# One transfer brings a row block and all 1024 columns of an adaLN vector, whose four column quarters are summed over eight row blocks in one PSUM bank

## The chip, the cores and the metric

One core of a Trainium2 chip runs the whole program. The metric is the device time of one execution in microseconds. TensorE (PE) multiplies, VectorE (DVE) and ScalarE (ACT) work on elements, GpSimd (POOL) does some of the rest, and the queue of SyncE (SP) issues nearly all transfers. Each engine works through its own row of instructions in the order in which they were put there.

## The reference, cut to what matters

A backbone of two layers over 512 latent tokens and 256 context tokens, 1024 wide, all in float32. Each layer has nine modulation vectors for the latents (from `c`) and nine for the context (from `c_ctx`):

```
ml = jnp.split(jax.nn.silu(c) @ mod_w[l] + mod_b[l], 9, axis=-1)       # mod_w[l]: 1024 x 9216
mc = jnp.split(jax.nn.silu(c_ctx) @ mod_w[l] + mod_b[l], 9, axis=-1)
x = x + 0.5 * ml[2] * _swiglu(_modnorm(x, norm_g[l, 0], ml[0], ml[1]), ffn_w1[l, 0], ffn_w2[l, 0])
...
def _modnorm(h, g, shift, scale): return _rmsnorm(h, g) * (1.0 + scale) + shift
```

Vectors 0, 3 and 6 of a layer shift, 1, 4 and 7 scale, and 2, 5 and 8 are gates, for the first FFN, the mixer and the second FFN. Layer 0 mixes with RWKV-7 and S5 scans, layer 1 with windowed attention. The context stream ends with its keys and values in layer 1.

## The kernel before, in words

Activations stand feature-major, as [128, 8, tokens]. A dense product holds a 128x128 block of weights and moves 256 or 512 tokens over it; `weight` (L349) brings the weights by SP, ScalarE rounds them to a high part (L328) and VectorE makes the low part (L329), and `mm3` (L365) multiplies three times for each block, on lines 370, 371 and 372. Weight transfers are named `wraw`.

The modulation vectors are made by `mod` (L208). The two conditioning vectors, context and latent, stand after silu in `sc` (L180), 32 columns wide with zeros beside them, so that one product serves both. `mod_w` is 75.5 MB in all, 18 vectors of 1024x1024. The kernel before goes by quarters of a vector's columns (`ch`, 256 columns each). For a quarter it brings four transfers `wt` (L222) of two row blocks and 256 columns each, 256 KB in rows of 1 KB:

```
for q in range(4):
    wt = self.mw.tile([128, 2, 256], F32, tag="mw", name="wt")
    nc.sync.dma_start(out=wt, in_=w[:, 2 * q:2 * q + 2, c0:c0 + 256])
    for r in range(2):
        nc.tensor.matmul(ps[32 * q:32 * q + 32, :256], self.sc[:, 2 * q + r, 2 - i:34 - i], wt[:, r, :], ...
```

The stationary side is 32 columns of `sc`, so a matmul takes one of four quarters of the array's columns and writes 32 partitions of PSUM. Transfer q's two matmuls (L224) go to the same partitions 32q to 32q+31; the four partial sums of a column block then stand on four partition groups. ScalarE copies them out (L228), two products with a selection matrix `sel` (L230) add the four and turn them into columns, and VectorE adds the bias (L234) and, for scales and gates, one step more (L237, L239). Up to three vectors share one bank (`i`, for calls with a tuple of vectors).

Vectors 0 and 1 of layer 0 come first, alone (`M_0` = 20 buffers); vectors 2, 3 and 4 are woven into the context's first FFN (`M_A` = 6 buffers), the next ten of both layers into the stage in which the context and the latents run as two streams (`M_B` = 2 buffers), and the last three into the two FFNs between the layers (4 buffers). `weave` (L1505) takes steps from several generators in turn, by the cost that each step yields. The program is built by a planner (`TCOPT`) that then orders each engine's instructions by its own costs, so that a line's place in the code doesn't fix its place in an engine's row.

Of the kernel before, what the change touches and what calls it, by code (L numbers as in the profile page):

```python
# [8 lines left out]
F32 = mybir.dt.float32  # L9
# [29 lines left out]
AHEAD = 3000  # L39
W_B = (2, 4)  # L40
M_B = 2
M_A = 6
LATE = (3, 20)
M_0 = 20
F_MOD = 1.8
F_LAT = 1.4
F_CTX = (2.4, 2.2)
# [13 lines left out]
class Net:  # L61
# [107 lines left out]
    def mod_vectors(self, pool):  # L169

        nc, a = self.nc, self.a
        self.vec, self.modv = {}, {}
        self.rows("vec0", [
            ("cc", a["c_ctx"].rearrange("(r p) -> r p", p=128)),
            ("c", a["c"].rearrange("b (r p) -> (b r) p", p=128)),
            ("mod_b0", a["mod_b"][0].rearrange("(r p) -> r p", p=128)),
            ("norm_g0", a["norm_g"][0].rearrange("s (r p) -> (s r) p", p=128)),
        ], pool)

        sc = self.const.tile([128, KB, 34], F32, name="sc")  # L180
# [3 lines left out]
        self.sc = sc  # L184

        self.sel = self.const.tile([128, 6], F32, name="sel")
        nc.vector.tensor_reduce(out=self.sel, in_=self.ident.rearrange("p (q i) -> p i q", q=4)[:, 0:6, :],
                                axis=mybir.AxisListType.X, op=ALU.add)

    def vectors(self, pool):  # L190
        a = self.a
# [13 lines left out]
        self.rows("vec2", [("mod_b1", a["mod_b"][1].rearrange("(r p) -> r p", p=128))], pool)  # L205


    def mod(self, l, *vs):  # L208

        nc = self.nc  # L210
        w = self.a["mod_w"][l].rearrange("(k p) n -> p k n", p=128)
        nv = len(vs)
        dst = self.const.tile([128, KB, nv, 2], F32, name=f"mod{l}_{vs[0]}")
        col = lambda nm, v, ks: self.vec[f"{nm}{l}"][:, v * KB + ks.start:v * KB + ks.stop].rearrange(
            "p (k i) -> p k i", i=1).to_broadcast([128, 2, 2])
        for ch in range(4):
            ps = self.bank("psmod") if self.start else self.norm_psum()
            for i, v in enumerate(vs):
                c0 = v * D + ch * 256
                for q in range(4):  # L220
                    wt = self.mw.tile([128, 2, 256], F32, tag="mw", name="wt")
                    nc.sync.dma_start(out=wt, in_=w[:, 2 * q:2 * q + 2, c0:c0 + 256])  # L222
                    for r in range(2):
                        nc.tensor.matmul(ps[32 * q:32 * q + 32, :256], self.sc[:, 2 * q + r, 2 - i:34 - i], wt[:, r, :],  # L224
                                         start=(i == 0 and r == 0), stop=(i == nv - 1 and r == 1))
                yield 3
            m = self.mw.tile([128, 256], F32, tag="modp", bufs=self.mp_bufs, name="modp")
# [3 lines left out]
            ks = slice(2 * ch, 2 * ch + 2)  # L231
            for i, v in enumerate(vs):
                o = dst[:, ks, i, :]
                nc.vector.tensor_tensor(out=o, in0=ps[:, 256:268].rearrange("p (k i v) -> p v k i", k=2, v=3)[:, i],  # L234
                                        in1=col("mod_b", v, ks), op=ALU.add)
                if v % 3 == 1:
                    nc.vector.scalar_tensor_tensor(out=o, in0=o, scalar=1.0, in1=col("norm_g", v // 3, ks), op0=ALU.add, op1=ALU.mult)  # L237
                elif v in (2, 8):
                    nc.vector.tensor_scalar(out=o, in0=o, scalar1=0.5, scalar2=None, op0=ALU.mult)  # L239
        for i, v in enumerate(vs):  # L240
            self.modv[l, v] = dst[:, :, i, :]


    def load_x(self, src, dst, pool):
# [14 lines left out]
    def sq_add(self, k, grp):  # L259

        nc = self.nc
        c0, n = grp
        if k == 0:
            self.ssum = getattr(self, "ssum", {})
            self.ssum[grp] = self.tp.tile([128, n], F32, tag=f"ss{c0}", bufs=1, name="ss")
            nc.scalar.activation(out=self.ssum[grp][:, :n], in_=self.xs(k, grp), func=ACTF.Square)
        else:
            sq = self.tp.tile([128, 256], F32, tag=f"sq{int(c0 >= CTX)}", bufs=1, name="sq")
            nc.scalar.activation(out=sq[:, :n], in_=self.xs(k, grp), func=ACTF.Square)
            nc.vector.tensor_tensor(out=self.ssum[grp][:, :n], in0=self.ssum[grp][:, :n], in1=sq[:, :n], op=ALU.add)  # L270

# [74 lines left out]
                                           in1=h[0][:, k, :].bitcast(F32), op0=ALU.add, op1=ALU.subtract)  # L346


    def weight(self, ap, pool=None, bufs=None):  # L349

        nc = self.nc
        _, kk, n = ap.shape
# [165 lines left out]
    def ab_tile(self, j, hs, consume, pool):  # L518

        c = slice(128 * j, 128 * j + 128)  # L520
        w, = self.weight(self.a["ab_in_w"][0].rearrange("(k p) n -> p k n", p=128)[:, :, c], pool, (1, self.ibufs[3]))
        for i, h in enumerate(hs):
            n = h[0].shape[2]
            ps = self.bank("pab")
# [969 lines left out]
def late(t, gen):  # L1494
    yield t
    yield from gen
# [8 lines left out]
def weave(*gens):  # L1505
    run(weave_gen(*gens))
# [16 lines left out]
def dit_kernel(ctx: ExitStack, tc: tile.TileContext, args, out):  # L1523
# [17 lines left out]

    def mods(l, *vs):
        for v in vs:
            yield from net.mod(l, *(v if isinstance(v, tuple) else (v,)))

    def scaled(gen, f):
        for t in gen:
# [95 lines left out]
    with net.psum(*PS), left("mix") as mp:  # L1643
        with net.mod_weights(M_A), net.weights(5, 5), right("r1") as rp:
# [10 lines left out]
            def more():  # L1655
# [10 lines left out]
            weave(ffn(0, 0, C, rp, FF_A), (late(LATE[0], mods(0, 2, (3, 4))), F_MOD), more())  # L1666
        with net.mod_weights(M_B), net.weights(*W_B):
            weave(ctx_stream(), lat_stream(), (chain(mods(0, (5, 6, 7), 8), mods(1, (0, 1, 2), (3, 4, 5))), 8.5))
    kp = ctx.enter_context(left("kv"))
    with net.psum(0, 2, m=4):  # L1670
        net.attn_setup()
        net.attn_tiles(kp)
        hc = tuple(xs.enter_context(right("hc" + p)).tile([128, KB, CTX], F32R, name=f"hc{p}") for p in "hl")
        with net.weights(*W_E, "left"), net.mod_weights(4), left("l12") as lp:
            def both():

                nh = []
# [16 lines left out]
            weave(both(), late(345, chain(mods(1, (6, 7, 8)), ctx_kv())))  # L1694
        xs.close()
    with net.psum(0, 2, 0, 2):
        late_w = ctx.enter_context(ExitStack())
# [61 lines left out]
```

## Time and profile before

| | |
|---|---|
| median of 3 runs | 3461.26 us (3457.91 to 3472.96) |
| the profiled execution | 3468.21 us, span 3466.4 us, mean granted clock 0.981 |
| PE busy, weight loads | 3362.3 us (97%), 2842.8 us (82%) |
| DVE, ACT, POOL busy | 1930.0 (56%), 1343.6 (39%), 331.8 us (10%) |
| moved | 463 MB, 134 GB/s over the span |
| transfers of `mod_w` | 288 of 256 KB |

A row of the timeline or of a group names line, engine, operation and tiles as out<-in. A float32 matmul that isn't rounded, as on line 224, leaves two records, its two passes. A matmul's duration includes its way through the array, so that records overlap; how fast PE works is read from start to start. All times are microseconds from the span's start.

### The profile page before, as it was taken

The page shows a single profiled execution, that of the slowest core. Times are in us where ns is not written, and L with a number is a line of the kernel's source. Part 1 is how long each engine was busy: PE and PEld are TensorE (multiplying, and loading weights), DVE is VectorE, ACT ScalarE, POOL GpSimd, SP SyncE. Part 2 cuts the span into 40 slices and gives each one's busy share as a digit, 9 for nine tenths or more (in the row PEclk, how much of TensorE's full clock was granted, in tenths as well). Part 3 has the DMA queues.
Part 4 walks back from the last instruction along what each step waited for, and adds up shares of the span by engine and source line. Part 5 has one row for each costly group of instructions (what it writes and reads, how often), then busy time and mean ns, then how long its engine had stood idle before and what let it go on. Part 6 is the DMA issues. An engine that isn't in the chain of part 4 may idle for free.

```text
span 3466.4 us, 64237 instructions
## 1 busy us (share of the span) xinstructions
PE 3362.3 (97%) x25657; PEld 2842.8 (82%) x25657; DVE 1930.0 (56%) x4366; ACT 1343.6 (39%) x2732; POOL 331.8 (10%) x474
## 2 busy tenths in 40 slices
PE   8999999999998999999999899999999999999999
PEld 6788888987787887788888888887788887698888
DVE  4676656354447678656856663334443368763333
ACT  3334534223234555433334542223432246652223
POOL 2680000400000005230000000000000000000000
PEclk9999999989999999999999999999999999999999
DMA  9756444435235556553444543334433323032222
GB/s 279 230 179 182 150 148 154 134 111 149 86 126 165 166 164 198 187 179 118 122 143 146 171 153 98 97 97 128 128 110 98 97 72 100 1 115 95 96 96 73
DMA packets 505989, 463.00 MB, mean 134 GB/s; under 512 B 74942, under 2 KB 486490, under 8 KB 505690
## 3 DMA queue, kind: packets, MB, share of 16 engines
q1 hardware_dynamic: 504160, 457.05, 42.5%
q8 instruction: 202, 3.31, 0.4%
q0 software_dynamic: 704, 1.16, 0.2%
q14 instruction: 97, 0.79, 0.1%
q10 hardware_dynamic: 826, 0.68, 0.1%
HBM read 422.71 MB, written 35.55 MB: 132 GB/s over the span
## 4 chain that ended last, share of the span: by engine, by line
PE 81%; DMA 8%; DVE 5%; ACT 2%; POOL 2%; issue 1%; SPq 0%; DVEq 0%; ACTq 0%; POOLq 0%
PE po L370 7%; PE po L371 7%; PE po L372 7%; PE pg L371 6%; PE pg L370 6%; PE pg L372 6%; PE pu L371 6%; PE pu L372 6%; PE pu L370 6%; PE psn L224 5%; DMA wraw<-in_ffn_w_dram 3%; DMA wt<-in_mod_w_dram 2%; DVE wl L329 2%; PE pgr L784 2%; PE py L865 2%
## 5 line engine op out<-in xcount | busy, mean ns | idle before, releaser
L328 ACT CAST wh<-wraw 128x512 fp32r<-128x512 f32 (+1 forms) x1172 | 661.1, 599 | 1421.8 <-PE po L371 352.9
L329 DVE TENSOR_TENSOR wl<-wraw,wh 128x512 fp32r<-128x512 f32 (+1 forms) x1172 | 795.1, 706 | 528.7 <-ACT wh L328 520.9
L370 PE MATMUL po<-ah,wh 128*128 128x256 f32 (+1 forms) x1520 | 488.8, 325 | 14.4 <-DVE sg L407 7.2
L371 PE MATMUL po<-al,wh 128*128 128x256 f32 (+1 forms) x1520 | 479.3, 316 | 5.2 <-DVE al L329 5.2
L370 PE MATMUL pg<-hh,wh 128*128 128x256 f32 (+1 forms) x1456 | 475.0, 326 | 6.7 <-ACT wh L328 4.4
L372 PE MATMUL po<-ah,wl 128*128 128x256 f32 (+1 forms) x1520 | 478.7, 316 | 0.0
L371 PE MATMUL pg<-hl,wh 128*128 128x256 f32 (+1 forms) x1456 | 472.3, 324 | 0.5 <-DVE hl L345 0.4
L372 PE MATMUL pg<-hh,wl 128*128 128x256 f32 (+1 forms) x1456 | 471.0, 323 | 0.5 <-DVE wl L329 0.5
L370 PE MATMUL pu<-hh,wh 128*128 128x256 f32 (+1 forms) x1456 | 467.5, 321 | 1.5 <-ACT wh L328 1.5
L372 PE MATMUL pu<-hh,wl 128*128 128x256 f32 (+1 forms) x1456 | 468.0, 321 | 0.5 <-DVE wl L329 0.5
L371 PE MATMUL pu<-hl,wh 128*128 128x256 f32 (+1 forms) x1456 | 466.0, 320 | 0.0
L370 PEld LDWEIGHTS po<-ah,wh 128*128 128x128 f32 x1520 | 290.9, 192 | 64.1 <-issue 11.2
L371 PEld LDWEIGHTS po<-al,wh 128*128 128x128 f32 x1520 | 292.9, 193 | 27.1 <-DVE al L329 6.3
L370 PEld LDWEIGHTS pg<-hh,wh 128*128 128x128 f32 x1456 | 281.3, 193 | 37.4 <-issue 6.8
L372 PEld LDWEIGHTS po<-ah,wl 128*128 128x128 f32 x1520 | 292.9, 193 | 19.8 <-issue 2.7
L371 PEld LDWEIGHTS pg<-hl,wh 128*128 128x128 f32 x1456 | 280.9, 193 | 28.0 <-issue 5.2
L372 PEld LDWEIGHTS pg<-hh,wl 128*128 128x128 f32 x1456 | 280.6, 193 | 24.1 <-issue 2.7
L370 PEld LDWEIGHTS pu<-hh,wh 128*128 128x128 f32 x1456 | 276.6, 190 | 26.7 <-issue 5.2
L372 PEld LDWEIGHTS pu<-hh,wl 128*128 128x128 f32 x1456 | 276.2, 190 | 25.4 <-issue 4.9
L371 PEld LDWEIGHTS pu<-hl,wh 128*128 128x128 f32 x1456 | 276.4, 190 | 24.5 <-issue 5.2
L440 DVE SCALAR_TENSOR_TENSOR xl<-po,mod,xl 128x256 f32<-128x256 f32 (+1 forms) x240 | 132.2, 553 | 259.4 <-PE po L372 258.7
L407 DVE TENSOR_TENSOR sg<-sg,pu 128x512 f32<-128x512 f32 x121 | 82.9, 685 | 266.2 <-PE pu L372 262.0
(423 smaller groups left out, 5245.7 us busy)
## 6 DMA issues: line engine op xcount, KB each, us to landing
wraw<-in_ffn_w_dram SPq DMA_DIRECT2D x436, 512.0 KB, 4.2
wt<-in_mod_w_dram SPq DMA_DIRECT2D x288, 256.0 KB, 3.9
wraw<-in_ab_in_w_dram SPq DMA_DIRECT2D x72, 256.0 KB, 3.5
wraw<-in_ffn_w_dram SPq DMA_DIRECT2D x52, 256.0 KB, 2.7
arbk<-arbk SPq DMA_DIRECT2D x24, 512.0 KB, 3.2
wraw<-in_ab_out_w_dram SPq DMA_DIRECT2D x24, 512.0 KB, 5.1
ebtl<-ebt SPq DMA_DIRECT2D x16, 512.0 KB, 3.6
ab<-arbk SPq DMA_DIRECT2D x16, 512.0 KB, 3.9
```

The costliest lines, as they stand in the source:

```text
L224: nc.tensor.matmul(ps[32 * q:32 * q + 32, :256], self.sc[:, 2 * q + r, 2 - i:34 - i], wt[:, r, :], start=(i == 0 and r == 0), stop=(i == n ...
L328: nc.scalar.copy(out=hi, in_=src)
L329: nc.vector.tensor_tensor(out=lo, in0=src, in1=hi.bitcast(F32), op=ALU.subtract)
L370: nc.tensor.matmul(ps, wh, xh, start=first, stop=False)
L371: nc.tensor.matmul(ps, wh, xl, start=False, stop=False)
L372: nc.tensor.matmul(ps, wl, xh, start=False, stop=last)
L407: nc.vector.tensor_tensor(out=sg, in0=sg, in1=pu, op=ALU.mult)
L440: nc.vector.scalar_tensor_tensor(out=xs, in0=ps[:, :n], scalar=gate[:, k, gi:gi + 1], in1=xs, op0=ALU.mult, op1=ALU.add)
L784: nc.tensor.matmul(pg[:, o:o + 128], ab[hs, e, 4 + 2 * c:6 + 2 * c, :], ab[hs, e, c:4:2, :], start=True, stop=True)
L865: nc.tensor.matmul(py2[64 * hh:64 * hh + 64, o:o + 64], lhs, rhs, start=n < 2, stop=n >= len(steps) - 2, tile_position=(0, 64 * hh))
```

## The change

`mod` makes one vector at a time. A transfer brings one row block k and all 1024 columns, 512 KB in rows of 4 KB. Its four matmuls share the stationary columns of `sc` and go to the four quarters of the array, one for each quarter of the vector's columns; each quarter is summed over the eight row blocks in PSUM. So the bank holds finished columns, quarter q on partitions 32q (context) and 32q+1 (latents). One copy, two transposes of 128x128 and one addition of the bias follow for the whole vector. A step of the weave is now one transfer with a cost of 1.5, before it was four with a cost of 3. Buffer counts are halved where there were more than two (20, 6 and 4 become 10, 3 and 2); `M_B` stays 2. The tag of the squares becomes one for both streams, and the mixer's staging tile shrinks to the 128 columns that it uses.

```diff
-M_A = 6
+M_A = 3
-M_0 = 20
+M_0 = 10
...
-            self.mp_bufs = 2 if n > 4 else 1
+            self.mp_bufs = 2 if n > 2 else 1
...
-        sc = self.const.tile([128, KB, 34], F32, name="sc")
+        sc = self.sc = self.const.tile([128, KB, 32], F32, name="sc")
...
-            nc.scalar.activation(out=sc[:, :, 2 + 3 * i], in_=self.vec[nm], func=ACTF.Silu)
...
-        self.sel = self.const.tile([128, 6], F32, name="sel")
...
+            nc.scalar.activation(out=sc[:, :, i], in_=self.vec[nm], func=ACTF.Silu)
...
-        for ch in range(4):
-            ps = self.bank("psmod") if self.start else self.norm_psum()
-            for i, v in enumerate(vs):
-                c0 = v * D + ch * 256
-                for q in range(4):
-                    wt = self.mw.tile([128, 2, 256], F32, tag="mw", name="wt")
-                    nc.sync.dma_start(out=wt, in_=w[:, 2 * q:2 * q + 2, c0:c0 + 256])
-                    for r in range(2):
-                        nc.tensor.matmul(ps[32 * q:32 * q + 32, :256], self.sc[:, 2 * q + r, 2 - i:34 - i], wt[:, r, :],
-                                         start=(i == 0 and r == 0), stop=(i == nv - 1 and r == 1))
-                yield 3
-            m = self.mw.tile([128, 256], F32, tag="modp", bufs=self.mp_bufs, name="modp")
-            nc.scalar.copy(out=m, in_=ps[:, :256])
-            for j in range(2):
-                nc.tensor.matmul(ps[:, 256 + 6 * j:262 + 6 * j], m[:, j * 128:(j + 1) * 128], self.sel, start=True, stop=True)
...
+        for k in range(KB):
+            wt = self.mw.tile([128, D], F32, tag="mw", name="wt")
+            nc.sync.dma_start(out=wt, in_=w[:, k, v * D:(v + 1) * D])
+            for q in range(4):
+                nc.tensor.matmul(ps[32 * q:32 * q + 32, :256], self.sc[:, k, :], wt[:, 256 * q:256 * q + 256],
+                                 start=k == 0, stop=k == KB - 1, tile_position=(0, 32 * q))
+            yield 1.5
+        m = self.mw.tile([128, 256], F32, tag="modp", bufs=self.mp_bufs, name="modp")
+        nc.scalar.copy(out=m, in_=ps[:, :256])
+        for j in range(2):
+            nc.tensor.transpose(ps[:, 256 + 128 * j:384 + 128 * j], m[:, j * 128:(j + 1) * 128], self.ident)
...
+        nc.vector.tensor_tensor(out=o, in0=ps[:, 256:512].rearrange("p (j q r) -> p q j r", j=2, q=4)[:, :, :, 0:2],
+                                in1=col("mod_b", v), op=ALU.add)
...
-            sq = self.tp.tile([128, 256], F32, tag=f"sq{int(c0 >= CTX)}", bufs=1, name="sq")
+            sq = self.tp.tile([128, 256], F32, tag="sq", bufs=1, name="sq")
...
-            raw = pool.tile([128, 4, 256], F32, tag="w", bufs=rb, name="wraw")
+            raw = pool.tile([128, 4, max(n, wide)], F32, tag="w", bufs=rb, name="wraw")
...
-            weave(ctx_stream(), lat_stream(), (chain(mods(0, (5, 6, 7), 8), mods(1, (0, 1, 2), (3, 4, 5))), 8.5))
+            weave(ctx_stream(), lat_stream(), (chain(mods(0, 5, 6, 7, 8), mods(1, 0, 1, 2, 3, 4, 5)), 8.5))
```

The changed kernel is 11 lines shorter, so its lines from L223 on count 10 or 11 less: transfers are L212, matmuls L214, copies L218 and transposes L220 there.

How the instructions stand, at three places. First PE's row at the program's start, from the first matmul of vector 0 (`psmod`: the bank of the first two vectors; `psn` below is the bank of the later ones and of the norms) to the first product of the FFN (`pg`). Before:

```order
L224 MATMUL psmod<-wt,sc 32x256 x18
L230 MATMUL psmod<-sel,modp 128x6 x2
L224 MATMUL psmod<-wt,sc 32x256 x2
L230 MATMUL psmod<-sel,modp 128x6 x2
L224 MATMUL psmod<-wt,sc 32x256 x8
L230 MATMUL psmod<-sel,modp 128x6 x2
```

Now:

```order
L214 MATMUL psmod<-wt,sc 32x256 x36
L279 MATMUL psn<-ones,ss 128x1 x2
L220 MATMUL psmod<-ident,modp 128x128 x2
L214 MATMUL psmod<-wt,sc 32x256 x4
L302 MATMUL psn<-dg,ones 128x128 x2
L214 MATMUL psmod<-wt,sc 32x256 x4
L214 MATMUL psn<-wt,sc 32x256 x4
L214 MATMUL psmod<-wt,sc 32x256 x20
L220 MATMUL psmod<-ident,modp 128x128 x2
L214 MATMUL psn<-wt,sc 32x256 x4
L359 MATMUL pg<-hh_281,wh 128x256
```

Before, the sums over quarters (`sel`) stand between the matmuls, two for each column block; now two pairs of transposes stand there, and 72 matmuls, those of 18 transfers, are ahead of the first product of the FFN.

Second, PE's row inside an FFN: in the context's first one (before), and in the one at the end of layer 0 (now).

```order
L370 MATMUL pu<-hh_354,wh 128x256
L224 MATMUL psn<-wt,sc 32x256 x2
L371 MATMUL pu<-hl_355,wh 128x256
L372 MATMUL pu<-hh_354,wl 128x256
L370 MATMUL pu<-hh_354,wh 128x256
L224 MATMUL psn<-wt,sc 32x256 x2
```

```order
L214 MATMUL psn<-wt,sc 32x256 x4
L359 MATMUL pu<-hh_27151,wh 128x512
L360 MATMUL pu<-hl_27152,wh 128x512
L361 MATMUL pu<-hh_27151,wl 128x512
L359 MATMUL pu<-hh_27151,wh 128x512
L214 MATMUL psn<-wt,sc 32x256 x4
```

A row of two was one transfer with both matmuls on one quarter of the array; a row of four is one transfer with a matmul on each quarter. Over the program, outside the bank of the first two vectors, PE's row had 106 rows of two matmuls of `mod`, 44 of four and 9 of eight; it now has 10 of two, 73 of four and 20 of eight.

Third, SP's queue at the start. Before:

```order
L249 DMA xraw<-in_ctx_dram 128x1024 x2
L222 DMA wt<-in_mod_w_dram 128x2x256 x36
L360 DMA wraw<-in_ffn_w_dram 128x4x256 x4
L222 DMA wt<-in_mod_w_dram 128x2x256 x2
L360 DMA wraw<-in_ffn_w_dram 128x4x256
L249 DMA xraw<-in_x_dram 128x1024 x2
```

Now:

```order
L238 DMA xraw<-in_ctx_dram 128x1024 x2
L212 DMA wt<-in_mod_w_dram 128x1024 x11
L349 DMA wraw<-in_ffn_w_dram 128x4x256 x2
L212 DMA wt<-in_mod_w_dram 128x1024 x6
L349 DMA wraw<-in_ffn_w_dram 128x4x256 x2
L212 DMA wt<-in_mod_w_dram 128x1024 x2
```

The first two weight transfers moved ahead: behind 11 of the new transfers, which are as many bytes as 22 of the old ones, instead of behind 36 of those.

## Rows read from the trace of the kernel before

**Rows 1.** The page: the span, the engines' busy time, the chain that ended last.

```profile
span 3466.4 us, 64237 instructions
PE 3362.3 (97%) x25657; PEld 2842.8 (82%) x25657; DVE 1930.0 (56%) x4366; ACT 1343.6 (39%) x2732; POOL 331.8 (10%) x474
...
PE 81%; DMA 8%; DVE 5%; ACT 2%; POOL 2%; issue 1%; SPq 0%; DVEq 0%; ACTq 0%; POOLq 0%
PE po L370 7%; PE po L371 7%; PE po L372 7%; PE pg L371 6%; PE pg L370 6%; PE pg L372 6%; PE pu L371 6%; PE pu L372 6%; PE pu L370 6%; PE psn L224 5%; DMA wraw<-in_ffn_w_dram 3%; DMA wt<-in_mod_w_dram 2%; DVE wl L329 2%; PE pgr L784 2%; PE py L865 2%
```

**Rows 2.** Windows: us, PE, PEld, DVE, ACT, POOL busy (count), clock, DMA share, GB/s.

```profile
40.00:300.00 260.00, 246.27 (x2029) 209.61 (x2030) 176.53 (x354) 94.78 (x196) 141.92 (x116) 0.97 0.72 218
300.00:1550.00 1250.00, 1214.51 (x10753) 1035.19 (x10753) 742.05 (x1796) 506.54 (x1032) 171.68 (x284) 0.97 0.49 151
...
2040.00:2500.00 460.00, 455.42 (x2324) 374.26 (x2324) 196.33 (x379) 151.06 (x288) 0.00 (x0) 0.99 0.37 115
```

**Rows 3.** The same windows: PE and PEld of line 224 alone.

```profile
0.00:40.00 40.00, 23.87 (x144) 10.15 (x144) 1.00 0.90 289
...
sum 3467.00, PE 226.83 PEld 80.58; mean PE 37.80 PEld 13.43
```

**Rows 4.** Timeline of PE, a lone matmul: start, us, line, tiles, records [idle before].

```profile
449.12 0.62 PE L224 MATMUL psn<-wt,sc 128*32 128x256 f32 x2
449.67 0.38 PE L370 MATMUL pab<-hh,wh 128*128 128x256 f32 x1
```

**Rows 5.** Timeline of PE, two matmuls on one quarter.

```profile
330.27 0.28 PE L371 MATMUL po<-al,wh 128*128 128x256 f32 x1
330.39 0.28 PE L372 MATMUL po<-ah,wl 128*128 128x256 f32 x1
330.60 1.05 PE L224 MATMUL psn<-wt,sc 128*32 128x256 f32 x4
331.58 0.39 PE L370 MATMUL po<-ah,wh 128*128 128x256 f32 x1
```

**Rows 6.** Timeline of PE, four matmuls, two on each of two quarters.

```profile
321.86 1.06 PE L224 MATMUL psn<-wt,sc 128*32 128x256 f32 x8
322.85 0.39 PE L370 MATMUL po<-ah,wh 128*128 128x256 f32 x1
```

**Rows 7.** Timeline of PE, eight matmuls, two on each of four quarters.

```profile
124.22 1.09 PE L224 MATMUL psn<-wt,sc 128*32 128x256 f32 x16
125.24 0.39 PE L370 MATMUL po<-ah,wh 128*128 128x256 f32 x1
```

**Rows 8.** Groups by line, PE: 40 to 2500 us, then 0 to 40.

```profile
L230 PE MATMUL psn<-sel,modp 128*128 128x6 f32 x112 | 14.8, 237 | 1.2 <-ACT modp L228 1.2
...
L253 PE MATMUL pst<-ident,xraw 128*128 128x128 f32 x16 | 4.1, 425 | 4.6 <-DMA xraw<-in_ctx_dram 4.5
```

**Rows 9.** Waits: PE for the transfers (us, times, longest).

```profile
PE psn L224 <- DMA wt<-in_mod_w_dram: 18.6, 12, 4.3
```

**Rows 10.** Timeline of PE, a group whose second transfer came late.

```profile
325.86 1.74 PE L224 MATMUL psn<-wt,sc 128*32 128x256 f32 x8 [0.60 <-DMA wt<-in_mod_w_dram]
327.54 0.39 PE L370 MATMUL po<-ah,wh 128*128 128x256 f32 x1
```

**Rows 11.** Transfers: queue, count, KB each, median us from issue to landing.

```profile
wt<-in_mod_w_dram SPq DMA_DIRECT2D x288, 256.0 KB, 3.9
wraw<-in_ffn_w_dram SPq DMA_DIRECT2D x436, 512.0 KB, 4.2
...
wraw<-in_ab_out_w_dram SPq DMA_DIRECT2D x24, 512.0 KB, 5.1
...
obl<-sout SPq DMA_DIRECT2D x8, 512.0 KB, 6.7
```

**Rows 12.** Timeline of the start: SP's queue, then PE.

```profile
33.47 4.07 SPq L360 DMA_DIRECT2D wraw<-in_ffn_w_dram  x4
...
40.91 0.39 PE L370 MATMUL pg<-hh,wh 128*128 128x256 f32 x1 [1.06 <-ACT wh L328]
```

More of the change, by code (lines that the diff above doesn't have):

```diff
@@ L205, in vectors, with mod @@
         self.rows("vec2", [("mod_b1", a["mod_b"][1].rearrange("(r p) -> r p", p=128))], pool)
-    def mod(self, l, *vs):
+    def mod(self, l, v):
         nc = self.nc
         w = self.a["mod_w"][l].rearrange("(k p) n -> p k n", p=128)
[L212 to L215, printed above, removed]
-        for ch in range(4):
-            ps = self.bank("psmod") if self.start else self.norm_psum()
-            for i, v in enumerate(vs):
-                c0 = v * D + ch * 256
-                for q in range(4):
-                    wt = self.mw.tile([128, 2, 256], F32, tag="mw", name="wt")
-                    nc.sync.dma_start(out=wt, in_=w[:, 2 * q:2 * q + 2, c0:c0 + 256])
-                    for r in range(2):
-                        nc.tensor.matmul(ps[32 * q:32 * q + 32, :256], self.sc[:, 2 * q + r, 2 - i:34 - i], wt[:, r, :],
-                                         start=(i == 0 and r == 0), stop=(i == nv - 1 and r == 1))
-                yield 3
-            m = self.mw.tile([128, 256], F32, tag="modp", bufs=self.mp_bufs, name="modp")
-            nc.scalar.copy(out=m, in_=ps[:, :256])
-            for j in range(2):
-                nc.tensor.matmul(ps[:, 256 + 6 * j:262 + 6 * j], m[:, j * 128:(j + 1) * 128], self.sel, start=True, stop=True)
[L231 to L241, printed above, removed]
@@ new lines, in mod @@
+        dst = self.const.tile([128, KB, 2], F32, name=f"mod{l}_{v}")
+        ps = self.bank("psmod") if self.start else self.norm_psum()
+        for k in range(KB):
[5 more added lines that the diff above has]
+            yield 1.5
@@ L244, in load_x @@
+        if v % 3 == 1:
+            nc.vector.scalar_tensor_tensor(out=o, in0=o, scalar=1.0, in1=col("norm_g", v // 3), op0=ALU.add, op1=ALU.mult)
+        elif v in (2, 8):
+            nc.vector.tensor_scalar(out=o, in0=o, scalar1=0.5, scalar2=None, op0=ALU.mult)
+        self.modv[l, v] = dst
     def load_x(self, src, dst, pool):
@@ L346, in modnorm, with weight @@
                                            in1=h[0][:, k, :].bitcast(F32), op0=ALU.add, op1=ALU.subtract)
-    def weight(self, ap, pool=None, bufs=None):
+    def weight(self, ap, pool=None, bufs=None, wide=256):
         nc = self.nc
@@ L520, in ab_tile @@
         c = slice(128 * j, 128 * j + 128)
-        w, = self.weight(self.a["ab_in_w"][0].rearrange("(k p) n -> p k n", p=128)[:, :, c], pool, (1, self.ibufs[3]))
+        w, = self.weight(self.a["ab_in_w"][0].rearrange("(k p) n -> p k n", p=128)[:, :, c], pool, (1, self.ibufs[3]), 128)
         for i, h in enumerate(hs):
@@ L1543, in mods @@
         for v in vs:
-            yield from net.mod(l, *(v if isinstance(v, tuple) else (v,)))
+            yield from net.mod(l, v)
     def scaled(gen, f):
@@ L1665, in more @@
                         yield 2
-            weave(ffn(0, 0, C, rp, FF_A), (late(LATE[0], mods(0, 2, (3, 4))), F_MOD), more())
+            weave(ffn(0, 0, C, rp, FF_A), (late(LATE[0], mods(0, 2, 3, 4)), F_MOD), more())
         with net.mod_weights(M_B), net.weights(*W_B):
-            weave(ctx_stream(), lat_stream(), (chain(mods(0, (5, 6, 7), 8), mods(1, (0, 1, 2), (3, 4, 5))), 8.5))
+            weave(ctx_stream(), lat_stream(), (chain(mods(0, 5, 6, 7, 8), mods(1, 0, 1, 2, 3, 4, 5)), 8.5))
     kp = ctx.enter_context(left("kv"))
@@ L1673, in dit_kernel @@
         hc = tuple(xs.enter_context(right("hc" + p)).tile([128, KB, CTX], F32R, name=f"hc{p}") for p in "hl")
-        with net.weights(*W_E, "left"), net.mod_weights(4), left("l12") as lp:
+        with net.weights(*W_E, "left"), net.mod_weights(2), left("l12") as lp:
             def both():
@@ L1693, in ctx_kv @@
                 yield from net.attn_kv(C, {G_CTX: hc}, lp)
-            weave(both(), late(345, chain(mods(1, (6, 7, 8)), ctx_kv())))
+            weave(both(), late(345, chain(mods(1, 6, 7, 8), ctx_kv())))
         xs.close()
```

6 lines of the change are left out of this document (3 added, 3 removed).

## The prediction

> **What bounds the kernel now.** I read the profile's own page first: TensorE (PE) is busy for 97% of a span of 3466.4 us, and it carries 81% of the chain of work that ended last; the matmuls of the adaLN vectors, line 224, are 5% of that chain and their transfers 2% [rows 1]. Then the windows by stage. Vectors are made in the start (0 to 40 us), the first context FFN (40 to 300), the stage of two streams (300 to 1550) and around 2040 to 2500, and in the last three of these PE is busy 246 of 260 us, 1214.5 of 1250 and 455 of 460 [rows 2]. Line 224 takes 226.8 us of PE, 23.9 of them in the start, so 203 us where PE is the bound [rows 3]. DMA is the bound only in the start (share 0.90) and is at 0.49 in the stage of streams [rows 2, 3].
>
> Then the timeline, for what a group of these matmuls costs PE. A row counts two records for each matmul; I count the time from a group's first start to the next line's first start. A lone matmul takes 449.67 - 449.12 = 0.55 us [rows 4]. Two, both on one quarter of the array's columns, take 331.58 - 330.60 = 0.98 [rows 5]. Four, two on each of two quarters, take 0.99 [rows 6]. Eight, two on each of four, take 1.02 [rows 7]. So it is the depth of the longest chain on one quarter that is paid: 0.12 us plus 0.43 per link, and another quarter beside it costs 0.01 to 0.02. A group also shifts its predecessor: 330.60 - 330.39 = 0.21 from the product before it, where products are 0.12 apart [rows 5].
>
> **The change part by part.** *The matmuls.* There are 576 before and after (18 vectors by 32). Before, the two matmuls of a transfer stand on the same quarter, so each transfer is a chain of two, and shares its time with another quarter only if the next transfer stands directly behind it and has landed. Now the four of a transfer stand on four quarters and the chain is one. Counted in the order of the instructions after the start: before, 185 groups, 165 of depth two and 20 of depth one; now 116 groups, 93 of depth one and 23 of depth two. Before: 165 x 0.98 + 20 x 0.55 = 172.7 us (the 203 us above hold besides this some 13 us of overlapping tails, 0.07 a group, and waits inside groups). No row shows four quarters at depth one: it lies between 0.55 [rows 4] and 1.02 [rows 7]; I take 0.55 + 3 x 0.013 = 0.59, by what a further quarter cost. Now: 93 x 0.59 + 23 x 1.02 = 78.3. Saved: **94 us** (at the upper bound, 116 x 1.02 = 118, it would be 54). The shift of 0.09 goes away for 185 - 116 = 69 groups: **6 us**.
>
> *The sum over quarters.* Line 230's products with the selection matrix take 14.8 us in 112 records, 28 pairs, after the start, 0.53 a pair [rows 8]. Instead come 16 pairs of 128x128 transposes; 16 such transposes took 4.1 us in the start, 0.26 each [rows 8], so 16 x 0.52 = 8. Saved: **6 us**. The copies on ScalarE and the small additions on VectorE fall from one per column block to one per vector; both engines are off the path, so they are nothing.
>
> *The waits for transfers.* PE was idle 18.6 us in 12 waits for these transfers [rows 9], and 0.60 us before a group whose halves then ran one after the other, in 1.68 us [rows 10]. Before, four transfers were issued in one step of the weave with two buffers to take them; now one is issued per step. The transfer doubles to 512 KB; those of that size land in 4.2 to 6.7 us, these of 256 KB in 3.9 [rows 11]. In the stage of streams 17 to 20 products stand between two groups now, some 20 x 0.12 + 0.2 = 2.6 us from group to group; with two buffers a transfer has two of these steps less its own 0.6 us, some 4.6 us, which the commonest of those rows (4.2) keeps. I take half the waits away: **9 us**, with 0 and 18 as ends.
>
> *The start.* The first product of the FFN begins at 40.91, after VectorE's and ScalarE's work and the weights that were issued behind 36 transfers from 33.47 on [rows 12]. Now weights are issued behind 11 of the new transfers, but PE's row still holds 18 of them ahead of the first product, so about the same bytes have to land at the same 289 GB/s [rows 3]. I count nothing; ends are 4 us either way. The scale vector is now whole only after its last transfer, where before its first block was ready early; this costs a copy, two transposes and an addition at the end of a start that waits for weights anyhow.
>
> *The rest* (one buffer for the squares instead of two, narrower staging in the mixer's input, buffer counts at equal bytes, the missing selection matrix) adds no work to PE, which has other work in its row; if that cover were gone, the shared buffer would cost one 0.4 us addition each time the two streams meet there. The order is also dealt anew far from the vectors, and this I can't price: PE's whole idle time is 3466 - 3362 = 104 us [rows 1], and I allow a quarter of it, 25 us, either way.
>
> Sum: 94 + 6 + 6 + 9 = 115 us of PE. Not all arrives, since weights and casts that were hidden under the slower PE will be late at times: PE is busy 95 to 99% of those stages and has 81% of the chain [rows 1, 2]; I take 0.9 between these. 115 x 0.9 = 104. The profiled execution took 3468.2 us (span 3466.4), 7 above the median of 3461.3; so 3364 on its scale, and **3358 us** against the median. About 0.5%, 17 us, is what a measurement of this kernel can tell from no change.
>
> **A rule against it.** The rows show that a group of two chains costs what one costs, although the program issues one chain whole before the other: 0.99 against 0.98 [rows 5, 6]. PE thus starts the second chain's work ahead of the first one's remainder. The Trainium skill, "TensorE: Matmul & The Clock Gate", section "The mechanism", says the contrary: "MATMULs are pc-monotone in start AND end — strict FIFO, no reordering". By that rule the saving of 94 us would be 9 (worked out as the first rival); by the rows it is 94, and this trace disagrees with the rule.
>
> **The rivals.** (1) *Matmuls start strictly in the order issued.* Each has two passes of 0.215, and only a second pass and the next one's first would overlap. A set of four is then 0.12 + 5 x 0.215 = 1.2 us, a double one 0.12 + 9 x 0.215 = 2.06: 93 x 1.2 + 23 x 2.06 = 159, a saving of 14 in place of 94, or, with the small starts between, 9. The whole is 9 + 21 = 30, x 0.9: **3434 us**. Against it: the 0.99 and the 1.02. For it: only where the second chain's data came late did the halves take 1.68 [rows 10], which any order explains. 0.07.
> (2) *The larger transfers eat half.* If they land in 5.4 us, past the 4.6 of room, each of the 125 outside the start is late by (5.4 - 4.6) / 2 = 0.4: 50 us, and **3407 us**. For it: 5.1 us for 512 KB of the mixer's output weights [rows 11]; DMA's low share speaks against. 0.16.
> (3) *Slower.* The same place, but with transfers that land as late as the slowest row, 6.7 us [rows 11], because SyncE's one queue holds weights back behind a transfer that waits for its buffer. Then (6.7 - 4.6) / 2 = 1.05 us x 125 = 131 against 104: 27 more, **3488 us**. It decides from a landing of 4.6 + 2 x 0.83 = 6.3 us on. Against it: 3.9 us today with half the bytes, and 12 waits in some 250 transfers. 0.05.
> (4) *More than forecast*: everything arrives, all 18.6 us of waits go, and the new order is lucky by 10: 3461 - 115 - 10 - 10 = **3326 us**. 0.12.
> That the matmuls don't stand in sets of four is excluded by the order, but for some ten places where a set is split.
>
> **How the numbers follow.** The forecast has the remaining 0.60, from 3330 to 3390. The range of 8 in 10 takes in half of (4) and most of (2): 3320 to 3425. Faster by over 0.5% (under 3444): the forecast, (4), (2) and most of (1), less what a bad new order spoils: 0.90. Within 0.5%: 0.06. Slower: 0.04.
>
> **What would show it.** Right: groups of eight records at about 0.66 us busy (0.59 to the next start); line 224's successor at some 90 to 105 us of PE over the span, the start included; PE's idle time for these transfers under 18 us; 18 copies on ScalarE; most of the gain in the stage of two streams, some in the first FFN and around 2040 to 2500, and nothing after it. Wrong: groups of eight at 1.2 us or more (rival 1); idle time before them at 0.4 us each or more (2, 3); or a gain on PE that comes back as waits for casts or weights in the stage of streams.

## The result and the profile after

The changed kernel took **3376.32 us** (median of 4 runs, 3374.25 to 3386.53) beside 3467.11 us of the kernel before in the same comparison (4 runs, 3457.91 to 3479.84): a ratio of **0.9742**, 95% interval 0.9701 to 0.9782. Ratios here are of the runs' means; times are medians. A second comparison, later on (run e8 below), gave 3377.45 us, 0.9743 (0.9719 to 0.9768). The forecast was 3358, its range 3320 to 3425. Both profiled executions stand 1.1 us above the medians of this comparison (3377.43 after, 3468.21 before), so they can be subtracted: the span fell by 91.0 us.

The page of the kernel after, with the answers to [rows 1]:

```profile
span 3375.4 us, 63644 instructions
...
PE 3220.2 (95%) x25549; PEld 2773.2 (82%) x25549; DVE 1928.8 (57%) x4281; ACT 1340.5 (40%) x2716; POOL 331.6 (10%) x474
...
PE 76%; DMA 10%; DVE 7%; ACT 3%; POOL 2%; issue 1%; SPq 0%; DVEq 0%; ACTq 0%; POOLq 0%
```

PE's busy time fell by 3362.3 - 3220.2 = 142.1 us, more than the span did, and its idle time rose from 104.1 to 155.2. PE's share of the chain that ended last fell from 81% to 76%, and DMA's and VectorE's rose by two points each. So PE was freed of more than arrived. Where that happened is read from windows of PE by stage. They are cut at the same places of both programs: the first product of the FFN (the start's end), a sum of squares at the end of the first context FFN, one at the end of the two streams, one before the tail, and the end. Columns: us, PE busy (records), clock, DMA share, GB/s. Before:

```profile
0.00:41.00 41.00, 33.07 (x202) 1.00 0.90 291
41.00:344.30 303.30, 289.11 (x2344) 0.98 0.68 208
344.30:2015.50 1671.20, 1618.73 (x15439) 0.97 0.49 149
2015.50:2467.50 452.00, 445.17 (x2353) 0.99 0.37 116
2467.50:3466.40 998.90, 976.16 (x5326) 0.99 0.27 87
```

After:

```profile
0.00:40.30 40.30, 19.95 (x173) 0.87 0.95 355
40.30:320.60 280.30, 263.21 (x2333) 0.97 0.71 222
320.60:1932.80 1612.20, 1527.16 (x15378) 0.97 0.50 153
1932.80:2369.10 436.30, 428.10 (x2309) 0.98 0.36 117
2369.10:3375.40 1006.30, 981.80 (x5360) 0.99 0.28 89
```

The stages became shorter by 0.7, 23.0, 59.0 and 15.7 us, and the last one 7.4 longer. In the start PE is busy 13 us less and the stage is only 0.7 us shorter: there the chain that ended last runs mostly through the transfers of `mod_w` and of weights, at a DMA share of 0.90 before and 0.95 now. The transfers moved 355 GB/s there, where the kernel before had 291; more bytes landed in the same time, and the first product came hardly earlier. In the two streams PE is busy 91.6 us less and idle 1671.2 - 1618.7 = 52.5 before, 85.0 after, so 32.5 of the 91.6 went into waits. Without the start, PE is busy 129.0 us less, and 90.3 arrived.

What a group of vectors' matmuls costs now: the timeline of PE (start, us, line, tiles, records), a group from two transfers, then one from one.

```profile
304.64 1.07 PE L214 MATMUL psn<-wt,sc 128*32 128x256 f32 x16
305.64 0.39 PE L359 MATMUL po<-ah,wh 128*128 128x256 f32 x1
...
309.65 0.64 PE L214 MATMUL psn<-wt,sc 128*32 128x256 f32 x8
310.22 0.38 PE L359 MATMUL po<-ah,wh 128*128 128x256 f32 x1
```

Four matmuls on four quarters hold PE for 310.22 - 309.65 = 0.57 us, eight for 1.00; before, four took 0.99 and two 0.98 [rows 5, 6]. The sums, in windows that hold the transfers' own instructions alone (PE and PEld; first before, where the sum is that of [rows 3], then after):

```profile
45.00:3500.00 3455.00, 202.96 (x1008) 70.43 (x1008) 0.98 0.42 130
```

```profile
45.00:3500.00 3455.00, 86.30 (x1000) 23.84 (x1000) 0.98 0.41 129
sum 3500.00, PE 99.24 PEld 28.99; mean PE 49.62 PEld 14.49
```

The groups by line that answer to [rows 8], on PE, and the copies on ACT:

```profile
L220 PE MATMUL psn<-ident,modp 128*128 128x128 f32 x32 | 6.2, 274 | 0.0
```

```profile
L218 ACT COPY modp<-psn 128x256 f32<-128x256 f32 x16 | 5.9, 371 | 15.2 <-PE psn L214 15.2
L218 ACT COPY modp<-psmod 128x256 f32<-128x256 f32 x2 | 0.7, 372 | 5.5 <-PE psmod L214 4.2 <-DMA rows<-in_rwkv_k_a_dram 1.3
```

The wait of [rows 9], and the transfers of [rows 11], after:

```profile
PE psn L214 <- DMA wt<-in_mod_w_dram: 8.8, 7, 2.9
```

```profile
wt<-in_mod_w_dram SPq DMA_DIRECT2D x144, 512.0 KB, 5.2
```

PE waits for these transfers 8.8 us in 7 places instead of 18.6 in 12, though a transfer takes 5.2 us to land. The new waits are of other kinds. In the stretch with the most of them (999.0 to 1471.8, before 1051.6 to 1558.5; PE is idle 46.4 us of it, before 25.8) the list of PE's waits (us in total, times, longest) has, after:

```profile
PE pl L688 <- DVE arbk L670: 9.0, 6, 4.7
PE po L360 <- DVE al L318: 8.4, 1, 8.4
PE pab L360 <- DVE hl L334: 7.1, 3, 3.9
PE pab L359 <- ACT hh L333: 6.2, 2, 5.2
```

and before:

```profile
PE psn L224 <- DMA wt<-in_mod_w_dram: 11.7, 6, 3.1
PE po L370 <- DVE sg L407: 2.7, 1, 2.7
```

Before, what PE waited for most was the vectors' own transfers. After, it is VectorE's and ScalarE's work on the scans (`arbk`) and on the operands of products (`al`, `hl`, `hh`), for which PE before waited 3.0 us in all in this stretch. The whole program shows the same. Behind the start, PE's waits add up to these us, by what ended them:

| | VectorE | ScalarE | transfers of `mod_w` | other transfers |
|---|---|---|---|---|
| before | 40.3 | 25.0 | 18.6 | 5.1 |
| after | 64.9 | 48.0 | 8.5 | 6.5 |
| after, another execution (e8) | 63.7 | 42.8 | 9.2 | 5.2 |

The waits for transfers fell, and those for VectorE and ScalarE rose by 24.6 and 23.0 us. The largest rises are in `wh` (the rounding of weights, 7.6 to 17.8), `hh` (4.0 to 14.6), `xc` (4.7 to 14.0) and `arbk` (3.9 to 10.9).

### The profile page after: what moved, and what is told of

Same layout as the page of the kernel before. It is cut to its first block, busy times and chain, and to the rows that moved or that the text cites. A ratio compares the mean times of both kernels' runs of the same rounds, so it can differ in the third digit from the quotient of the medians.

```text
span 3375.4 us, 63644 instructions
## 1 busy us (share of the span) xinstructions
PE 3220.2 (95%) x25549; PEld 2773.2 (82%) x25549; DVE 1928.8 (57%) x4281; ACT 1340.5 (40%) x2716; POOL 331.6 (10%) x474
## 4 chain that ended last, share of the span: by engine, by line
PE 76%; DMA 10%; DVE 7%; ACT 3%; POOL 2%; issue 1%; SPq 0%; DVEq 0%; ACTq 0%; POOLq 0%
PE po L359 7%; PE po L360 7%; PE po L361 7%; PE pg L359 6%; PE pg L360 6%; PE pg L361 6%; PE pu L359 6%; PE pu L361 6%; PE pu L360 6%; DVE wl L318 3%; DMA wraw<-in_ffn_w_dram 3%; DMA wt<-in_mod_w_dram 2%; PE psn L214 2%; PE py L854 2%; PE pgr L773 1%
## 5 line engine op out<-in xcount | busy, mean ns | idle before, releaser
L361 PEld LDWEIGHTS pu<-hh,wl 128*128 128x128 f32 x1456 | 277.7, 191 | 21.7 <-issue 2.2
```

The costliest lines, as they stand in the source:

```text
L361: nc.tensor.matmul(ps, wl, xh, start=False, stop=last)
```

## The experiments

Three theories were held against each other. **P**: the time comes from the depth of the chains on PE; what the change does to transfers matters little. **T**: it comes from the transfers' form (half as many, in rows of 4 KB, one in a step). **O**: it comes from the order, which is dealt anew for the whole program. The first four runs were compared with 3467.55 us of the kernel before (7 runs).

**e1, the depth alone, with the transfers of before.** The two matmuls of a transfer go to two quarters of the array instead of one; transfers, copies and products with `sel` stay.

```diff
+                        c = 32 * ((2 * q + r) % 4)
-                        nc.tensor.matmul(ps[32 * q:32 * q + 32, :256], ...
-                                         start=(i == 0 and r == 0), stop=(i == nv - 1 and r == 1))
+                        nc.tensor.matmul(ps[c:c + 32, :256], ...
+                                         start=(i == 0 and q < 2), stop=(i == nv - 1 and q > 1), tile_position=(0, c))
```

> The kernel before with one part of the change alone: the two matmuls of a transfer go to two quarters of the array instead of one; transfers (288 of 256 KB), the weave, buffers, selection products and counts stay. In its order some 172 groups after the start have depth one and 13 more, where before 165 had two. Theory P (the depth of the chain on a quarter is what PE pays): 172 x 0.57 + 11 x 1.0 + 2 x 1.43 = 112 us instead of 172.7, so 61 us of PE less and, with 0.67 to 0.9 of it arriving, a kernel 41 to 55 us faster than before (3412 to 3426). Theory T (the larger transfer, one per step, with fewer waits, makes the gain): no change, within 15 us of before. Theory O (what the planner's new order happens to give makes most of it): anything between 30 us slower and 30 us faster, whatever PE's time on these matmuls.

Measured: 3418.23 us (3411.99 to 3420.97, 4 runs), 0.9842 (0.9813 to 0.9870): 49 us, over half of the change's gain. The line is L225 here. In the timeline, a group on four quarters, then one on two:

```profile
311.97 0.64 PE L225 MATMUL psn<-wt,sc 128*32 128x256 f32 x8
...
317.78 0.62 PE L225 MATMUL psn<-wt,sc 128*32 128x256 f32 x4
```

PE's time for the transfers' instructions, by window, and its wait for them:

```profile
45.00:3500.00 3455.00, 127.72 (x1008) 0.98 0.42 130
```

```profile
PE psn L225 <- DMA wt<-in_mod_w_dram: 19.9, 17, 6.3
```

A chain of one costs the same on one quarter (0.62, [rows 4]), two (0.62) and four (0.64). PE has 75 us less of these matmuls and waits for the transfers as long as before. P holds, and T can't be the whole: the transfers are those of before. (The trace is of e1's fastest run.)

**e2, the change without the depth.** All of the change stands, but the four matmuls of a transfer go to two quarters, 512 columns of the bank each; two copies and four half-height transposes follow.

```diff
-                nc.tensor.matmul(ps[32 * q:32 * q + 32, :256], ...
+                c, h = 32 * (q // 2), 256 * (q % 2)
+                nc.tensor.matmul(ps[c:c + 32, h:h + 256], ...
...
```

> The changed kernel with the packing alone undone: the same 512 KB transfers and weave, but the four matmuls of a transfer go to two quarters, two each, with 512 columns of the bank; two copies and four transposes of half the height per vector in place of one and two. Its order has 86 groups of depth two, 22 of four, 11 of one, 4 of three, 2 of six, where the changed kernel has 96 of one and 23 of two. Theory P: 144 us for these groups instead of 78, and some 7 us for transposes, so 74 us of PE more and 50 to 66 us slower than the changed kernel (3425 to 3442). Theory T: within 15 us of the changed kernel. Theory O: anything within 30 us of it.

Measured: 3423.66 us (3420.85 to 3437.38, 4 runs), 0.9857 (0.9825 to 0.9889), just under P's figure. The trace is of its slowest run (3437.38). The line is L215 here; by timeline, window and waits, a group of two transfers and one of one, the time of PE (and PEld), and the wait:

```profile
316.86 1.94 PE L215 MATMUL psn<-wt,sc 128*32 128x256 f32 x16
318.73 0.39 PE L362 MATMUL po<-ah,wh 128*128 128x256 f32 x1
...
325.83 1.06 PE L215 MATMUL psn<-wt,sc 128*32 128x256 f32 x8
```

```profile
45.00:3500.00 3455.00, 151.77 (x1000) 58.47 (x1000) 0.98 0.41 129
```

```profile
PE psn L215 <- DMA wt<-in_mod_w_dram: 10.5, 8, 2.5
```

The four matmuls take 1.06 again, as before the change [rows 6], and 47 of the 91 us are gone. Two such transfers in a row make a chain of four links on each of two quarters: 318.73 - 316.86 = 1.87 us to the next start, where 0.12 + 4 x 0.43 gives 1.84. So the prediction's cost by depth holds at four links too. What is left, 44 us, belongs to the rest: a transfer now brings four matmuls, which stand two and two on two quarters and can't be parted, where a pair alone used to take as long (202.96 falls to 151.77 at the same depth); the wait shrinks, and there are fewer sums over quarters. The depth alone, with the old transfers, gave 49 (e1); the form alone gave 44: about half each of the 91. P was right that chains on PE decide, and T that the form counts, though more by PE's time on the matmuls (51 us less) than by the waits for transfers (18.6 to 10.5).

**e3, the start.** In the kernel after, PE's row stands idle in the start before the norm's sum of squares. The edit gives the squares of the start two buffers.

```diff
-            sq = self.tp.tile([128, 256], F32, tag="sq", bufs=1, name="sq")
+            sq = (self.rp if self.start else self.tp).tile([128, 256], F32, tag="sq", bufs=1 + self.start, name="sq")
...
-            net.start = True
+            net.start, net.rp = True, rp
```

> The changed kernel with a second buffer for the squares of the context in the start alone. In the changed kernel PE stands idle 6.0 us at about 20 us for the sum of squares, with seven transfers of matmuls behind that wait, and its first FFN product begins at 40.3, hardly before the 40.9 of the kernel before. If that chain of squares and additions holds the start: the wait shrinks to under 3 us, the first product begins 3 to 6 us earlier, and the time falls by 3 to 6 us. If the weights or the transfers hold it: the first product stays at 40 and the time within 5 us. Theory O: the time can move by up to 30 us for an edit that touches only the first 40 us.

Measured: 3371.28 us (3364.57 to 3375.89, 4 runs), 0.9707 (0.9679 to 0.9736). The timeline of PE, of the kernel after:

```profile
26.12 1.01 PE L279 MATMUL psn<-ones,ss 128*128 128x1 f32 x4 [5.95 <-DVE ss L259]
...
40.31 0.39 PE L359 MATMUL pg<-hh,wh 128*128 128x256 f32 x1 [2.46 <-ACT hh L333]
```

and of e3:

```profile
21.17 0.61 PE L279 MATMUL psn<-ones,ss 128*128 128x1 f32 x4 [2.39 <-DVE ss L259]
...
38.20 0.58 PE L359 MATMUL pg<-hh,wh 128*128 128x256 f32 x1
```

The sum came 5 us earlier and the first product of the FFN 2.1, less than the 3 to 6 that were expected of it. The medians differ by 5.0 us, less than the runs of each kernel do, so the pair was run again:

**e8 and e9, the pair once more, five rounds on one chip.**

> The kernel after, unchanged, as the other half of a pair with the next run on the same chip. Both theories: 3370 to 3382 us, 0.971 to 0.976 of the kernel before.

> The kernel after with two buffers for the squares in the start, once more, beside the kernel after itself. Theory S (the sum of squares holds up PE's row in the start, and what it gives back, 2.1 us at the first product of the FFN, stays until the end): 2 to 6 us less than the run beside it. Theory 0 (the start is paid back in later waits, the 5 us of the first comparison were chance): within 2 us of it, either way.

Measured: e8, the kernel after, 3377.45 us (3372.31 to 3387.18, 5 runs), 0.9743 (0.9719 to 0.9768); e9 3373.55 us (3372.42 to 3379.11, 4 runs), 0.9735 (0.9714 to 0.9755). The second buffer is 3.9 us ahead again, within theory S. The sign is the same twice, and the traces show the place twice (the first product at 40.55 in e8 and 38.48 in e9), but the intervals overlap: that the 2 us at the first product stay until the end is likely and not shown.

**e4, a new order alone.** In the kernel after, the cost at which the vectors are woven into the two streams becomes 9.5; only the order moves.

```diff
-            weave(ctx_stream(), lat_stream(), (chain(mods(0, 5, 6, 7, 8), mods(1, 0, 1, 2, 3, 4, 5)), 8.5))
+            weave(ctx_stream(), lat_stream(), (chain(mods(0, 5, 6, 7, 8), mods(1, 0, 1, 2, 3, 4, 5)), 9.5))
```

> The changed kernel with the weave's factor for the vectors in the stage of two streams at 9.5 instead of 8.5: the same instructions, dealt a little later. It measures what a new order alone is worth. Theory O: it differs from the changed kernel by 15 to 30 us either way. Theories P and T: within 10 us.

Measured: 3374.60 us (3370.67 to 3378.80, 4 runs), 0.9719 (0.9691 to 0.9746). 1.7 us is no difference that these runs can tell. As far as this one edit goes, O moves the time by a few us, not by tens.

**e5, still less of PE's work.** The kernel after, with 64 of each quarter's 256 columns multiplied and copied four times: three quarters of each vector's columns are left out.

```diff
-                nc.tensor.matmul(ps[32 * q:32 * q + 32, :256], self.sc[:, k, :], wt[:, 256 * q:256 * q + 256],
+                nc.tensor.matmul(ps[32 * q:32 * q + 32, :64], self.sc[:, k, :], wt[:, 256 * q:256 * q + 64],
...
```

> The kernel after, with only the first 64 of each quarter's 256 columns multiplied; they are copied four times into the tile that is transposed. It leaves out three quarters of each vector's columns, the transfers and all counts of instructions stay. On PE the vectors' matmuls should fall from 86 us after the start to some 35 to 45, about 45 us less. Theory P (the time follows what PE is freed of, of which 0.6 to 0.7 arrives, as in the runs before): 27 to 32 us less than the kernel after, 3343 to 3351. Theory B (what the change freed has laid bare another bound, casts and weights, so that PE's time no longer counts): under 12 us less, 3364 to 3378. Theory F (PE's time counts in full, and the third that was lost came from the new transfers or order): 42 us or more less, under 3336.

Measured: 3360.02 us (3353.57 to 3366.47, 4 runs), 0.9682 (0.9656 to 0.9708), beside 3468.66 us of the kernel before (13 runs, as for e6 and e7). PE's time for the transfers' instructions, its wait for the transfers, then PE in the start and behind it:

```profile
45.00:3500.00 3455.00, 44.13 (x1000) 0.98 0.41 129
```

```profile
PE psn L214 <- DMA wt<-in_mod_w_dram: 17.5, 13, 2.5
```

```profile
0.00:37.70 37.70, 13.76 (x174) 1.00 0.96 362
37.70:3358.60 3320.90, 3183.35 (x25380) 0.97 0.43 135
```

The vectors' matmuls fell by 42 us, and the time by 16: none of the three theories, between P (27 to 32) and B (under 12). Behind the start PE as a whole is busy only 3200.3 - 3183.4 = 16.9 us less, so its other work took some 25 us longer by the records. The clock explains part of that: laid over PE's busy time behind the start, the stretches at 1.2 GHz cost 72 us in this execution and 57 in that of the kernel after (66 in e8), so some 15 of the 25. The other 10 stay open. PE also waits for the vectors' own transfers again, 17.5 us in 13 places where the kernel after has 8.8 in 7. What the run does say is that the next 42 us of these matmuls are worth less than the last ones.

**e6, e3 and e4 together.**

> The kernel after with both edits that were tried one by one: two buffers for the squares in the start (3371.3 alone) and the weave's cost for the vectors at 9.5 in place of 8.5 (3374.6 alone), against 3376.3 without. If they act on different stages and add up: some 3369 us, 3365 to 3373, with the first product of the FFN at 38 to 39 us. If the order that is dealt anew decides more than either edit: anywhere from 3362 to 3382, with the difference in stages after 45 us that neither edit touches.

Measured: 3371.86 us (3368.44 to 3382.62, 4 runs), 0.9722 (0.9698 to 0.9746), the first product at 38.77: inside the first figure, and no better than e3 alone. It is inside the second figure too, so it doesn't decide between the two.

**e7, the two small edits in the kernel before.** One buffer for the squares and the narrow staging; every engine's row is that of before.

> The kernel before with only the two small edits of the change that its prediction counted at nothing: one buffer for the squares of both streams, and the mixer's input staged in tiles of 128 columns. Every engine's row stays as before. Theory N (they cost nothing; the 7 us that the kernel after takes longer behind 2467 us come from the order dealt anew): 3461 to 3473 us, and the stage behind the second group of vectors' products (2467 us) 998 to 1001 us long. Theory W (the shared buffer is waited for in the last stage): that stage 1004 to 1008 us long, the whole 3472 to 3478.

Measured: 3470.76 us (3461.61 to 3475.78, 8 runs), 0.9995 (0.9977 to 1.0014): they cost nothing, as the prediction had it. The last stage, by the same windows, lies between both theories' figures:

```profile
2471.60:3473.80 1002.20, 979.19 (x5326) 0.99 0.27 87
```

The row is that of before, the stage 3.3 us longer: so much it can move between two executions. Of the 7.4 us after the change the windows show another part: 5360 records instead of 5326, and 44 fewer in the stage ahead. Of the 34 that the new order put behind the mark, 20 are products of 512 tokens, which start 0.23 us apart in this stage, so 4.6 us; most of the others are the vectors' own. So the tail's 7 us can be a shifted boundary and scatter; the stage ahead, which gained 15.7, then gave them.

**The runs together.** For each profiled execution, without its start: PE busy by the windows, idle as the rest of the stretch. The execution of e1 was its fastest run, those of e2 and e6 their slowest.

| | PE busy, us | PE idle, us | mean clock of the span |
|---|---|---|---|
| before | 3329.2 | 96.2 | 0.981 |
| e7, before with the small edits | 3333.7 | 100.7 | 0.980 |
| e2, after at depth two | 3280.4 | 110.4 | 0.977 |
| e1, before on two quarters | 3266.4 | 104.4 | 0.977 |
| e6 | 3216.7 | 125.3 | 0.974 |
| e4 | 3213.3 | 118.0 | 0.975 |
| after, another execution (e8) | 3205.5 | 130.1 | 0.974 |
| after | 3200.3 | 134.8 | 0.977 |
| e5, 64 columns | 3183.4 | 137.5 | 0.975 |

Whichever part of the change takes time from PE, its idle time goes up, by some 8 us for the first 63 (e1) and by 30 for the next 66 (from e1 to after). A new order moves it by up to 17 (e4 against after) with little change of the total; two executions of the kernel after differ by 5 in either column.

## Why the prediction was right, and where it was off

The time fell as forecast, inside the range, 18 us above the likeliest value. The mechanism on PE was right; that the number came so close is luck, since two of its terms were wrong in opposite directions. Step by step:

*The matmuls, 94 us: the mechanism right, the size low.* The depth of the longest chain is what is paid: 0.57 for a set of four where 0.59 was estimated, 1.00 for a double one where 1.02 stood. After the change the records of line 214 behind the start hold 86.30 us; less 0.07 of tail for each of 116 groups that is 78.2, and 78.3 was forecast. The miss is in the part before: 202.96 less 185 x 0.07 is 190, where the counted groups gave 172.7. The 17 us between were set aside as waits inside groups, of which the change would save nothing. Counted group by group in the trace of before, 16 of them sit in 13 of the 185 groups, and they are not idle time: in some the chains ran one after the other because a transfer came late, as in [rows 10], and others ran at the lower clock (1.2 GHz), which by the clock's records makes some 7 of the 16 (e7, with the order of before, has 16 and 6 again). The same count leaves 3 us in the kernel after, nearly all by the clock: a set of four has one transfer and can't be cut in two by a late one. So the term is 112 us.

*The sum over quarters, 6 us:* 14.8 - 6.2 = 8.6. *The switches, 6 us:* not measured alone. With 112 that makes 127 (6 of them unmeasured), and PE's busy time behind the start fell by 129.0.

*The waits for transfers, 9 us:* 18.6 - 8.8 = 9.8. The room of 4.6 us that a transfer was given proved too strict: they land in 5.2, and yet PE waits in 7 places only. What carries the others was not tried.

*The start, nothing:* 0.7 us, by 13 us less of PE and as many more waits, though not at the 289 GB/s that the prediction held fixed but at 355; what of that is due to the longer rows was not tried. The prediction looked for the cost of the squares' buffer where the two streams meet. In the start the shared tag changes nothing: only the context's squares are made there, and they had one buffer before too. What is new is PE's row. Before, PE was at the vectors up to the norm's sum:

```profile
23.16 1.05 PE L224 MATMUL psmod<-wt,sc 128*32 128x256 f32 x4
24.14 0.61 PE L290 MATMUL psn<-ones,ss 128*128 128x1 f32 x4
```

Now the sum stands between two groups, PE is done with the first of them at 20.2, and it waits 5.95 us for the squares; a second buffer takes 3.6 us off that (e3). The single buffer costs some 2 us at the first product (e3, e9); at the end the medians differ by 5.0 and 3.9, within the scatter.

*The share that arrives, 0.9: this step failed.* PE was freed of 129.0 us of work and 9.8 of waits, 139 in all against 115 forecast, and 90.3 arrived, 0.65. The 48.5 us between are other idle time: PE's idle time behind the start rose by 134.8 - 96.2 = 38.6 although 9.8 of it had gone. Had 0.9 held, 125 would have arrived. The two errors, a term too small and a share too large, met in the middle by luck: 104 forecast, 91 measured. The prediction had named the place (weights and casts that were hidden under the slower PE), and such waits were one of its own signs of being wrong; it had taken the share from how busy PE was, 95 to 99%, and its 81% of the chain. Those tell what PE does now, not how soon the other engines' work is ready once PE comes earlier. The waits by kind account for the 48.5 us: 24.6 more for VectorE, 23.0 more for ScalarE. e1 beside the kernel after suggests that the first 63 us of PE's time arrive more fully than the next 66: 54.6 and 35.7 us by these executions, 49 and 42 by the medians. That PE's waits shifted to VectorE and ScalarE is seen in two executions of each order (e7, with that of before, has 37.9 and 25.5); that a faster VectorE or ScalarE there would bring the time back was not tried.

*The rivals.* (1) Strict order, 3434: refuted, sets of four take 0.57 and not 1.2. The records of the set at 309.65 show how: four passes start within 20 ns, and four more 0.24 us later, as if each matmul's second pass came behind the first passes of all four. The prediction weighed a rule of the Trainium skill ("TensorE: Matmul & The Clock Gate", section "The mechanism") and read it pass by pass; read so, e1's 0.62 on two quarters and the kernel after's 0.57 disagree with it. Read for whole matmuls it doesn't give the rival's 1.2 us: in a set of four, first starts and last ends can both be in the order issued. Where the rule fails even so is a group of two chains, issued one whole before the other as the kernel's loop has it: before, at 321.86 [rows 6], two passes start 13 ns apart and the next only 0.23 us later, so the second chain's first matmul starts ahead of the first chain's second (e2's 1.06 is the same). (2) and (3), larger transfers that eat the gain: refuted by 8.8 us of waits and by e1, where transfers half as large are waited for 19.9 us. (4), everything arrives: not so, by the 0.65.

## What to carry to other kernels

With few stationary columns, spread the matmuls of one loaded tile over the quarters of the array's columns: here PE paid for the longest chain on one quarter, and the others came nearly free (0.55 us for one, 0.57 for four); a set that hangs on a single transfer also can't be cut by a late one. When an engine that is busy 97% is freed of 4% of the span, don't read the share that arrives from that 97%: look at what the other engines deliver just in time in the same stretch, and add up PE's waits by the engine that ends them before and after. Here 0.65 arrived, and the second half of the saving seems to be worth less than the first. What costs nothing in one order (a single buffer) can stand in PE's way in the next, so costs of nothing are to be looked at again in the trace after.

## What the runs showed of the hardware that was not expected

In the start the clock follows PE's waits. In the kernel after, PE's windows of 2 us (us, PE busy, clock) show:

```profile
18.00:20.00 2.00, 1.71 (x32) 1.00 1.01 412
20.00:22.00 2.00, 0.17 (x4) 1.00 1.06 377
22.00:24.00 2.00, 0.00 (x0) 1.00 1.09 372
24.00:26.00 2.00, 0.00 (x0) 0.50 1.02 391
26.00:28.00 2.00, 1.71 (x10) 0.50 0.98 357
28.00:30.00 2.00, 1.00 (x8) 0.50 0.98 327
...
32.00:34.00 2.00, 2.00 (x25) 0.50 0.98 344
34.00:36.00 2.00, 2.00 (x36) 0.94 1.08 396
```

PE has nothing to do from 20.2 on; the granted clock falls from 2.4 to 1.2 GHz at 24, stays there while PE works on in pieces, and is back after PE had been at work without a gap. The sum of squares at 26.12 pays for it: its four small matmuls take 1.01 us, and 0.61 in e3, where they ran ahead of the fall of the clock (at 21.7). In e9 the clock fell at 20.7, as they began, and they took 1.01 again. Over the span the missing clock is 3466.4 x (1 - 0.981) = 66 us of full speed before, 78 after, and 88 in e8. Of the 12 us between the two compared executions 5 lie in the start, 40.3 x (1 - 0.87). Behind it the part that falls on PE's busy time is 57 us in both (66 in e8), so the 129.0 us above owe nothing to the clock in this pair. Two executions of one kernel can differ by as much: e3 took 3364.57 us at 0.979 and 3375.89 at 0.974.

The cost of a chain is also plainer than expected: two, four and eight records of a chain of one take 0.62, 0.62 and 0.64 us of busy time, whatever the number of quarters.
